# Opening attention's pools and strands inside the recurrence's scheduling loop, one pool at a time

## The chip, the core and the metric

The kernel runs on one core of a Trainium2 chip. It is one launch. The time is that of the device, in microseconds (us), for the whole launch; it is given as the median of three runs. One execution was also profiled, and every row below is from that one. The core's engines each work through their own instructions in order: PE (TensorE, matrix products; PEld are its weight loads), ACT (ScalarE), DVE (VectorE), POOL (GpSimd) and SP (SyncE, which here issues every transfer between memory and the core).

## What is computed

A decoder layer over 528 positions (16 meta tokens and 512 inputs) of width 1024. Cut to what matters here:

```
h      = rms_norm(concat(meta, x)) ; proj = h @ w_in          # 1024 -> 8480 columns
o_rwkv = rwkv7_mix(proj[:, 0:3360]) @ rwkv_w_o                 # 16 heads of 64, a recurrence over time
o_diff = diff_attention(proj[:, 3360:6432]) @ diff_w_o         # 8 heads; each the difference of two causal softmaxes
gates  = sigmoid(proj[:, 6432:8480])                           # 2 x 1024
h_res  = h_res + (gates0 * o_rwkv + gates1 * o_diff) @ w_out
h_res  = h_res + square(relu(rms_norm(h_res) @ mlp_w1)) @ mlp_w2
out    = rms_norm(h_res)[16:]
```

All of it is float32. A wide product is done as three products of rounded halves (high x high, high x low, low x high).

## The kernel before

**Stages.** First the input is normed and turned (lines 130 to 252). Then comes a part whose order is planned by hand (lines 270 to 1525, inside `mstack`): the recurrence and attention. Then the end of attention's output product, the merge, `w_out` and the MLP (from line 1530).

**The planner.** Each piece of work is a Python generator, a *strand*, that yields operations (`Op`, line 282) or conditions to wait for. `run` (line 1125) takes again and again the strand whose next operation could start first by estimated costs and times, with a small handicap by `RANK` (line 1115) and a limit (`debt`) on how much PE work of short bursts may go ahead of dense work. What it picks is written into the engines' queues in that order. The estimates choose the order alone; on the chip each instruction waits for what it really needs. A tile's slot is known to the planner as free at the time in `touched`.

**Dense work.** `loader`, `splitter`, `wide` and `evacuation` (lines 574 to 641) run the wide products: a job is one tile of 128 output columns. `loader` issues the weights in four transfers of two row tiles, `splitter` makes their halves on ACT and POOL (`whi`, `wlo`), `wide` runs the matmuls (tile `fil`) and `evacuation` empties the result. Jobs needed by the recurrence are in `need`; all the others (attention's q, k, v columns and 16 gate jobs) are in `other` and serve as filling between the recurrence's short matmuls. `HELD = 6` (line 531) keeps the last six gate jobs back until `closed[0]` is set.

**The recurrence** goes over four groups of four heads. Of group `grp`, `operands` (line 1102) makes the operands, `substitution` and `inverse` the triangular inverses (done: `inverted[grp]`), `chain` (line 889) the nine steps in series (done: `chained[grp]`), and `finish` (line 1002) norms the result, adds the bonus, multiplies by the gate and stores it to `or_d` (done: `finished[grp]`). Two groups are in work at a time. The pools are `pd`, `pe`, `pr` in SBUF and `psg` (tiles `gm0`, `gm1`), `psr` (`sm`, `py`), `psj` and `psf` in PSUM, two banks each.

**The seam.** `run()` of the recurrence returns when only the four strands of dense work are left (line 1133), which is after `finish` of group 3. All its pools are then closed, attention's pools opened (line 1169), the six held jobs put around the products with `rwkv_w_o` (`job_o`, eight jobs) and `diff_w_o` (`job_d`, eight jobs of half length, over the first four heads), and a second `run(True)` starts with attention's strands (line 1521).

**Attention.** `fetching` (line 1201) loads q, k, v and the rotated rows of a head, `loading` (1233) turns v on PE and makes the halves of q, k and v (done: `H[hd]`); four heads may be loaded and not yet attended. `vf` has one buffer, so the v of a head is loaded after the head before it is done. `scoring` and `softmax` (1291 to 1343) make the scores (`sc`) and their exponentials (`p`), `differences` and `weighting` the weighted values (`attended[hd]`), `norms` the norm and the store to `od_d`. `outs` (1455) reloads the recurrence's result from `or_d` and makes its halves (`oh`, `ol`) for `job_o`, after `soft[3]`; `reloads` (1496) does so for `job_d` (`dh`, `dl`) after the eight `job_o`.

The planner's and the dense work's key lines:

```python
elif len(other) > (0 if closed[0] else HELD):          # 564
    yield other.pop(0)()
...
if not last and all(s[1].gi_code.co_name in LASTING for s in strands):   # 1133
    return
...
other[:] = held[:len(held) - 1] + [lambda m=m: job_o(m) for m in range(NT)] + held[len(held) - 1:] + [...job_d...]   # 1519
closed[0] = True
for g in (setup(), fetching(), loading(), scoring(), differences(), weighting(), norms(), outs(), reloads(), gates_ahead()):
    fork(g)
run(True)
```

Of the kernel before, what the change touches and what calls it, by code (L numbers as in the profile page):

```python
# [10 lines left out]
F32 = mybir.dt.float32  # L11
F32R = mybir.dt.float32r
# [67 lines left out]
def hybrid_layer(ctx: ExitStack, tc: tile.TileContext, ins, out):  # L80
# [99 lines left out]
    psj = pstack.enter_context(tc.tile_pool(name="psj", bufs=1, space=PSUM))  # L180
# [94 lines left out]
    with tc.tile_pool(name="pd", bufs=1) as pd_, tc.tile_pool(name="pe", bufs=1) as pe_, tc.tile_pool(name="pr", bufs=1) as pr_, tc.tile_pool(name="psg", bufs=2, space=PSUM) as psg, tc.tile_pool(name="psr", bufs=2, space=PSUM) as psr:  # L275
# [35 lines left out]
        class Pool:  # L311

            def __init__(self, pool):
                self.pool = pool

            def tile(self, shape, dtype, tag=None, name=None, bufs=1):
                tag = tag or name
                t = self.pool.tile(shape, dtype, tag=tag, name=name, bufs=bufs)
                key = (id(self.pool), tag)
                n = turns.get(key, 0)  # L320
                turns[key] = n + 1
                s = slot_of[t.tensor.name] = (*key, n % bufs)
                fresh[t.tensor.name] = touched.get(s, 0.0)
                return t

        pd_, pe_, pr_, psg, psr, early_, gpool_, psf_, psj_ = (Pool(x) for x in (pd_, pe_, pr_, psg, psr, early, gpool, psf, psj))
# [204 lines left out]
        HELD = 6  # L531
# [357 lines left out]
        def chain(G):  # L889
# [3 lines left out]
            Yg = G["Yg"] = pr_.tile([P, 2, NC - 1, C], F32, tag="Yg", name="Yg")  # L893
# [108 lines left out]
        def finish(grp, G):  # L1002
# [3 lines left out]
            var = pr_.tile([P, 16], F32, tag="var", name="var")  # L1006
            rsh, vs = ([projected[w, grp, pr] for pr in range(2)] for w in "rv")

            def norm(i, n):

                for j in range(0, n, 8):
                    o = 8 * i + j
                    ysq = pr_.tile([P, S], F32, tag="ft", name="ysq", bufs=2).rearrange("p (a b) -> p a b", b=C)
# [10 lines left out]
            def bonus(pr):  # L1024
                r = rsh[pr]
                hi = pr_.tile([P, S], F32R, tag="ft", name="bhi", bufs=2)
                yield act(out=hi, in_=r, func=AF.Copy)
                lo = pr_.tile([P, S], F32R, tag="ft", name="blo", bufs=2)
# [9 lines left out]
            def gate_rows(pr):  # L1038
                g2 = ins["rwkv_g2"][0, :, P * (2 * grp + pr):P * (2 * grp + pr + 1)]
                raw = pr_.tile([P, 2, P], F32, tag="graw", name="graw")  # L1040
# [5 lines left out]
            def gate_halves(raw):  # L1046
                g2h = pr_.tile([P, 2, P], F32R, tag="g2h", name="g2h")
                g2l = pr_.tile([P, P], F32R, tag="g2l", name="g2l")
# [13 lines left out]
            for pr in range(2):  # L1062
# [7 lines left out]
                yf = pr_.tile([P, S], F32, tag="ft", name="yf", bufs=2)  # L1070
# [31 lines left out]
        def operands():  # L1102

            for grp in range(4):
# [11 lines left out]
                "fetching": 1, "loading": 2, "scoring": 1, "softmax": 1, "differences": 1, "weighting": 1, "norms": 2, "merging": 2, "outs": 2, "reloads": 2, "gates_ahead": 2, "setup": 0}  # L1116
        LASTING = ("loader", "splitter", "wide", "evacuation")
# [7 lines left out]
        def run(last=False):  # L1125

            while True:
# [5 lines left out]
                if not last and all(s[1].gi_code.co_name in LASTING for s in strands):  # L1133
                    return
# [26 lines left out]
        for g in (loader(), splitter(), wide(), evacuation(), states(), operands(), endings()):  # L1161
            fork(g)
        run()

    estack.close()
    pstack.close()


    with tc.tile_pool(name="pa1", bufs=1, reuse_waits="tile") as pa1, tc.tile_pool(name="pa2", bufs=1, reuse_waits="tile") as pa2, tc.tile_pool(name="pa", bufs=2, reuse_waits="tile") as pa, tc.tile_pool(name="psa", bufs=1, space=PSUM, reuse_waits="tile") as psa, ExitStack() as ostack:
        with tc.using_default_side("right"):  # L1170
            po = ostack.enter_context(tc.tile_pool(name="po", bufs=1, reuse_waits="tile"))
        pa1, pa2, pa, psa, po = (Pool(x) for x in (pa1, pa2, pa, psa, po))
        BANKS.update(sc=(psa, ("sc0", "sc1", "sc2")), sm=(psa, ("sm0", "sm1")), o=(psa, ("o",)))

        ka = pa1.tile([P, KN - K_CAU], F32, name="ka")
        ones = pa.tile([P, 1], F32, name="ones")
        rope = ka[:, K_COS - K_CAU:KN - K_CAU].rearrange("p (a t) -> p a t", a=2)
        cau, idb = (pa.tile([P, P], BF16, name=n) for n in ("cau", "idb"))


        vms = [pa.tile([P, P], F32R, tag=f"vm{i}", name=f"vm{i}") for i in range(4)]

        kzs = [pa.tile([P, 2, M], F32R, tag=f"kz{i}", name=f"kz{i}") for i in range(4)]
        am = pa.tile([P, 256], F32R, name="am")
        H, soft, sums_of, mixed, turned, attended, normed, heads_out = {}, {}, {}, {}, {}, {}, {}, []

        def setup():
            yield dma(out=ka, in_=ins["consts"][:, K_CAU:KN])
            yield dve("memset", ones, 1.0)
            yield dve("tensor_copy", idb, ident)  # L1190
            for t in vms + [am] + [x.rearrange("p a b -> p (a b)") for x in kzs]:
                yield dve("tensor_scalar", out=t, in0=par[:, 0:1].to_broadcast((P, t.shape[-1])), scalar1=0.0, scalar2=None, op0=ALU.mult)
            yield dve("tensor_copy", cau, ka[:, 0:P])
# [7 lines left out]
        def fetching():  # L1201

            for hp in range(4):
# [7 lines left out]
                yield dve("tensor_tensor", out=xx, in0=xx, in1=rope[:, 0, :], op=ALU.mult)  # L1211
# [521 lines left out]
```

## Time and profile before

| what | us |
|---|---|
| median of 3 runs (1294.82 to 1300.45) | 1298.17 |
| profiled execution | 1297.67 |
| its span, first to last instruction | 1295.6 |
| PE busy | 1202.4 (93%) |
| DVE busy | 704.8 (54%) |
| ACT busy | 646.0 (50%) |
| POOL busy | 401.4 (31%) |

A row of the timeline gives the start, the duration, the engine, the line of the kernel, the operation, what it writes and reads, the shape and how many were merged into the row; in brackets the engine's idle time before it and what ended that. L118, L359, L365 and L373 are lines of helpers, so the tiles' names tell which piece of work it is. "Granted clock" (PEclk) is the share of TensorE's full clock of 2.4 GHz that was granted; it is 1.0 or 0.5 (1.2 GHz), and values between are means over a stretch.

### The profile page before, as it was taken

How to read it: one execution, taken by the hardware profiler on the slowest of the kernel's cores; microseconds unless marked ns; L12 is line 12 of the kernel's file. 1: busy time of each engine (PE TensorE's matmuls, PEld its weight loads, DVE VectorE, ACT ScalarE, POOL GpSimd, SP SyncE). 2: the span in 40 equal slices, each digit the busy share in tenths (PEclk: the TensorE clock that was granted, in tenths of full speed). 3: DMA queues.
4: the chain of work that ended last, by engine and by line, in shares of the span. 5: the costliest groups of instructions: out<-in, count | busy, mean ns of one | idle time of the engine just before them, and what ended most of it. 6: DMA issues, size and time to landing. Idle time of an engine off the chain costs nothing.

```text
span 1295.6 us, 22932 instructions
## 1 busy us (share of the span) xinstructions
PE 1202.4 (93%) x8297; PEld 992.8 (77%) x8297; DVE 704.8 (54%) x1387; ACT 646.0 (50%) x1561; POOL 401.4 (31%) x619
## 2 busy tenths in 40 slices
PE   5999899989999899999687999998899999999997
PEld 5999787878878787776465777776788888888886
DVE  4546845694359845923357877745544332444233
ACT  6675466645656475454277878523344311234222
POOL 3555434542435343533154565520000000000000
PEclk9999899998989899999697999999999999999999
DMA  3322322341224222331564453686233223332222
GB/s 123 88 70 77 91 67 80 91 128 49 60 56 115 57 72 75 103 95 54 145 182 132 148 160 110 224 294 215 81 83 97 98 98 98 98 90 91 96 98 81
DMA packets 166469, 138.18 MB, mean 107 GB/s; under 512 B 12641, under 2 KB 130756, under 8 KB 166356
## 3 DMA queue, kind: packets, MB, share of 16 engines
q1 hardware_dynamic: 166356, 136.73, 35.5%
q8 instruction: 65, 1.06, 0.3%
q14 instruction: 48, 0.39, 0.1%
HBM read 112.36 MB, written 23.23 MB: 105 GB/s over the span
## 4 chain that ended last, share of the span: by engine, by line
PE 59%; DVE 14%; DMA 5%; ACT 4%; issue 3%; SPq 1%; POOL 1%; POOLq 0%; DVEq 0%; ACTq 0%
PE b L118 30%; PE fil L118 18%; PE gm L118 4%; PE sm L118 3%; DVE Tm L365 3%; DVE tmp L365 2%; PE py L118 2%; SPq L373 1%; DMA rl<-th_d 1%; PE sm L394 1%; PE sc L118 1%; DMA xx<-xr_d 1%; PE o L118 1%; DVE mx L365 1%; DVE AR L365 1%
## 5 line engine op out<-in xcount | busy, mean ns | idle before, releaser
L365 POOL TENSOR_TENSOR wlo<-wraw,whi 128x256 fp32r<-128x256 f32 x316 | 249.7, 796 | 346.1 <-ACT whi L359 276.0
L118 PE MATMUL fil<-hh,whi 128*128 128x264 f32 (+2 forms) x880 | 195.0, 326 | 14.2 <-ACT whi L359 9.2
L115 DVE TENSOR_TENSOR wlo<-wraw,whi 128x1024 fp32r<-128x1024 f32 x72 | 88.2, 1224 | 219.6 <-ACT whi L114 219.6
L118 PE MATMUL b<-whi,x 128*128 128x512 f32 x640 | 200.0, 392 | 4.7 <-ACT whi L114 4.7
L114 ACT ACTIVATE whi<-wraw 128x1024 fp32r<-128x1024 f32 x72 | 76.2, 1060 | 251.2 <-PE b L118 234.8
L118 PE MATMUL fil<-hh,wlo 128*128 128x264 f32 (+2 forms) x880 | 192.4, 322 | 0.0
L118 PE MATMUL fil<-hl,whi 128*128 128x264 f32 (+2 forms) x880 | 189.6, 321 | 0.0
L359 ACT ACTIVATE whi<-wraw 128x256 fp32r<-128x256 f32 x316 | 129.0, 413 | 102.6 <-PE fil L118 48.7
L118 PE MATMUL b<-h,whi 128*128 128x512 f32 x512 | 160.6, 395 | 0.8 <-DVE h L1690 0.8
L118 PEld LDWEIGHTS fil<-hh,whi 128*128 128x128 f32 x880 | 136.1, 195 | 28.1 <-ACT whi L359 12.3
L118 PEld LDWEIGHTS b<-whi,x 128*128 128x128 f32 x640 | 120.4, 189 | 31.9 <-ACT whi L114 6.0
L118 PEld LDWEIGHTS fil<-hh,wlo 128*128 128x128 f32 x880 | 135.5, 193 | 11.0 <-POOL wlo L365 0.5
L118 PEld LDWEIGHTS fil<-hl,whi 128*128 128x128 f32 x880 | 135.9, 194 | 10.4 <-issue 0.5
L1670 POOL TENSOR_TENSOR sums<-sums,halfs 128x1 f32<-128x1 f32 x8 | 5.3, 665 | 425.7 <-DVE sums L1669 365.5
L118 PE MATMUL b<-wlo,x 128*128 128x512 f32 x320 | 126.2, 394 | 0.0
L118 PEld LDWEIGHTS b<-h,whi 128*128 128x128 f32 x512 | 96.4, 188 | 23.4 <-DVE h L1690 1.0
L118 PE MATMUL b<-h,wlo 128*128 128x512 f32 x256 | 101.0, 394 | 0.0
L118 PEld LDWEIGHTS b<-wlo,x 128*128 128x128 f32 x320 | 60.6, 189 | 13.9 <-DVE wlo L115 1.1
L365 DVE TENSOR_TENSOR Tm<-Tm,tmp 128x31 f32<-128x31 f32 (+15 forms) x124 | 56.6, 456 | 3.1
L118 PEld LDWEIGHTS b<-h,wlo 128*128 128x128 f32 x256 | 48.3, 188 | 11.3
L365 DVE TENSOR_TENSOR tmp<-Dm,Tm 128x31 f32<-128x31 f32 (+15 forms) x124 | 54.0, 436 | 3.5
L365 DVE COPY suv<-sm 64x128 f32<-64x128 f32 x36 | 10.5, 292 | 73.9 <-ACT suv L359 73.8
(287 smaller groups left out, 2001.4 us busy)
## 6 DMA issues: line engine op xcount, KB each, us to landing
wraw<-in_w_in_dram SPq DMA_DIRECT2D x268, 128.0 KB
wraw<-in_mlp_w_dram SPq DMA_DIRECT2D x64, 512.0 KB
oth<-th_d SPq DMA_DIRECT2D x24, 256.0 KB
th_d<-th SPq DMA_DIRECT2D x16, 256.0 KB
wraw<-in_rwkv_w_o_dram SPq DMA_DIRECT2D x32, 128.0 KB
th_d<-oth SPq DMA_DIRECT2D x16, 256.0 KB
rl<-th_d SPq DMA_DIRECT2D x16, 256.0 KB
wraw<-in_w_out_dram SPq DMA_DIRECT2D x8, 512.0 KB
```

Source lines behind the costliest of these rows:

```text
L114: nc.scalar.activation(out=hi, in_=src, func=AF.Copy)
L115: (lo_eng or nc.vector).tensor_tensor(out=lo, in0=src, in1=hi.bitcast(F32), op=ALU.subtract)
L118: return nc.tensor.matmul(o, lhsT=l, rhs=r, start=start, stop=stop)
L359: lambda: nc.scalar.activation(out=out, in_=in_, func=func, scale=scale, **more), aps(in_, scale, bias), aps(out, accum_out))
L365: return Op(eng, SLOW * (cost or fixed + each * n), lambda: getattr(unit, name)(*args, **kw), aps(*args[1:], *(v for k, v in kw.items() if ...
L373: return Op("SP", 0.45, lambda: nc.sync.dma_start(out=out, in_=in_), aps(in_), [out], 2.4)
L394: self.todo.append(lambda: nc.tensor.transpose(out=o, in_=i, identity=idn))
L1670: nc.gpsimd.tensor_tensor(out=o, in0=o, in1=halfs[:, 0:1], op=ALU.pow)
```

## The change

There is one `run()` now. A strand `opening` closes the recurrence's pools and opens attention's, one after the other:

- After `inverted[3]` and `chained[2]`, that is when the chain of group 3 is about to start, `pd` and `pe` are closed and `pa1` and `pa2` opened in their place; `setup`, `fetching` and `loading` start. `loading` uses the banks `gm0`, `gm1` (was: `sm0`, `sm1` of attention's own pool).
- After `chained[3]`, `pr`, `psj` and `psr` are closed, `pa` and `psa` opened; the held jobs are let go, and scoring, differences, weighting, norms, outs, reloads and gates_ahead start. `finish` of group 3 has its tiles in a pool `pf` that stays and runs beside them.
- `NH = 3` heads may be loaded ahead (was 4), `HELD = 4` (was 6).
- `po` is gone. The halves for `job_o` lie in the recurrence's tiles (`place`), and `outs` starts after `finished[3]` (was `soft[3]`); those for `job_d` lie in attention's input tiles, and `reloads` starts after `H[7]` (was: after the eight `job_o`). Their reload buffer and that of the gates is `ft`, shared with `finish`.
- `pd`, `pe`, later `pa1`, `pa2`, lie on the right side of SBUF. In PSUM `psg` now lies where `psj` lay; `psj` and `psr` are opened after the first stage and marked free for the planner at 5.0.

```diff
-        HELD = 6
+        HELD = 4
...
-            def __init__(self, pool):
-                self.pool = pool
+            def __init__(self, pool=None):
+                self.pool, self.since = pool, 0.0
+
+            def open(self, stack, name, after, **kw):
+                self.pool = stack.enter_context(tc.tile_pool(name=name, bufs=1, reuse_waits="tile", **kw))
+                self.since = max(t for s, t in touched.items() if s[0] in [id(x.pool) for x in after])
...
+        touched[id(psj_.pool), "pj2", 0] = touched[id(psj_.pool), "pj3", 0] = 5.0
...
-                if not last and all(s[1].gi_code.co_name in LASTING for s in strands):
-                    return
...
         def loading():
             for hd in range(8):
-                while hd > 3 and hd - 4 not in attended:
-                    yield until(attended, hd - 4)
+                while hd >= NH and hd - NH not in attended:
+                    yield until(attended, hd - NH)
...
-            pv = yield from bank("sm")
+            pv = yield from bank("gm")
...
+        PLACES = [("vs", PT, 4)] * 4 + [("rsh", S, 4)] * 4 + [("ks", PT, 2)] * 2 + [(n, PT, 1) for n in ("w_hi", "a_hi", "wa_lo")] + [(n, S, 1) for n in ("g_hi", "g_lo", "g_end")]
...
         def outs():
-            yield until(soft, 3)
+            yield until(finished, 3)
             for k in range(NT):
-                t = po.tile([P, S], F32, tag="ol", name="ol", bufs=2)
+                t = pf_.tile([P, S], F32, tag="ft", name="ol", bufs=2)
                 yield dma(out=t, in_=or_d[:, k, :])
-                hi, lo = (po.tile([P, S], F32R, tag=f"o{x}{k}", name=f"o{x}{k}") for x in "hl")
+                hi, lo = place(2 * k), place(2 * k + 1)
...
         def reloads():
-            yield until(gates, *range(NT))
+            yield until(H, 7)
...
+        def opening():
+
+            yield until(inverted, 3)
+            yield until(chained, 2)
+            dstack.close()
+            with tc.using_default_side("right"):
+                pa1.open(astack, "pa1", (pd_, pe_))
+                pa2.open(astack, "pa2", (pd_, pe_))
+            for g in (setup(), fetching(), loading()):
+                fork(g)
+            yield until(chained, 3)
+            while not (dfree[2] and dfree[3]):
+                yield lambda: dfree[2] and dfree[3]
+            rstack.close()
+            bstack.close()
+            pa.open(ostack, "pa", (pr_, pd_))
+            psa.open(ostack, "psa", (psj_, psr), space=PSUM)
+            BANKS.update(sc=(psa, ("sc0", "sc1", "sc2")), o=(psa, ("o",)))
+            assert len(other) == HELD
+            held = other[:]
+            other[:] = held[:HELD - 1] + [lambda m=m: job_o(m) for m in range(NT)] + held[HELD - 1:] + [lambda m=m: job_d(m) for m in range(NT)]
+            closed[0] = True
+            for g in (setup_pa(), scoring(), differences(), weighting(), norms(), outs(), reloads(), gates_ahead()):
+                fork(g)
+
+        for g in (loader(), splitter(), wide(), evacuation(), states(), operands(), endings(), opening()):
             fork(g)
-        run(True)
+        run()
```

## Rows read from the trace of the kernel before

**Rows 1.** The page's 40 slices of 32.4 us: PE's busy tenths, granted clock.
```profile
PE   5999899989999899999687999998899999999997
PEclk9999899998989899999697999999999999999999
```

**Rows 2.** Busy time by stretch: stretch and length; PE, PEld, DVE, ACT, POOL; clock; DMA.
```profile
560.00:610.30 50.30, 49.95 (x513) 34.24 (x512) 13.70 (x45) 26.34 (x80) 16.74 (x31) 1.00 0.23 64
610.30:632.70 22.40, 10.99 (x81) 6.83 (x79) 10.46 (x29) 5.51 (x12) 3.63 (x4) 0.68 0.21 63
632.70:656.70 24.00, 20.75 (x76) 15.43 (x77) 4.83 (x8) 10.46 (x23) 11.37 (x16) 0.87 0.73 215
656.70:720.00 63.30, 53.29 (x276) 38.86 (x274) 50.09 (x117) 49.34 (x134) 30.43 (x48) 0.87 0.48 146
720.00:850.30 130.30, 122.39 (x715) 95.57 (x716) 92.94 (x228) 92.30 (x251) 75.15 (x106) 1.00 0.55 171
850.30:903.00 52.70, 46.36 (x190) 36.14 (x189) 28.42 (x40) 13.83 (x20) 3.05 (x2) 0.97 0.80 271
```

**Rows 3.** Timeline at the seam: the recurrence's last result to the first scores.
```profile
627.90 0.69 DVE L365 TENSOR_TENSOR yf<-gm,yf 128x512 f32<-128x512 f32 x1 [0.60 <-PE gm L118]
632.25 1.03 ACT L359 ACTIVATE whi<-wraw 128x256 fp32r<-128x256 f32 x3 [5.89 <-DMA wraw<-in_w_in_dram]
632.72 1.22 PE L118 MATMUL fil<-hh,whi 128*128 128x512 f32 x2 [4.86 <-ACT whi L359]
641.60 1.84 SPq L373 DMA_DIRECT2D qk<-xx  x3
656.67 0.34 PE L118 MATMUL sc<-k,q 128*128 128x144 f32 x2
```

**Rows 4.** Timeline: chain 2's end, finish 2's end, inverse 3's end, chain 3's end.
```profile
526.66 0.28 ACT L359 ACTIVATE Yg<-py 128x128 f32<-128x128 f32 x1 [0.60 <-PE py L118]
...
564.59 0.34 SPq L373 DMA_DIRECT2D or_d<-yf  x1
...
566.26 1.36 ACT L359 ACTIVATE TT<-Td 32x576 f32<-32x576 f32 x2
...
610.03 0.28 ACT L359 ACTIVATE Yg<-py 128x128 f32<-128x128 f32 x1 [1.25 <-PE py L118]
```

**Rows 5.** Attention's loads: by tile (ns min/median/max, first to last start), and timeline rows.
```profile
L359 ACT ACTIVATE k<-qk x32: 627/642/647, 650.5 to 798.3; 64x528 fp32r<-64x528 f32 x32
L365 POOL TENSOR_TENSOR klo<-qk,k x16: 1292/1323/1665, 651.3 to 800.0; 64x528 fp32r<-64x528 f32 x16
L359 ACT ACTIVATE of<-o x8: 573/588/598, 691.5 to 834.8; 128x512 f32<-128x512 f32 x8
...
782.52 0.20 POOL L365 CAST kz<-klo 64x16 fp32r<-64x16 f32 x1
782.62 0.34 PE L118 MATMUL sc<-k,q 128*128 128x144 f32 x2
784.88 0.63 PE L394 MATMUL sm<-kc,vf 128*128 128x128 f32 x4 [0.25 <-DMA vf<-v_d]
```

**Rows 6.** By tile: the halves of the reloaded results, of `or_d` and of `od_d`.
```profile
L359 ACT ACTIVATE oh<-ol x8: 613/631/638, 682.2 to 713.8; 128x512 fp32r<-128x512 f32 x8
L365 DVE TENSOR_TENSOR ol<-ol,oh x8: 674/687/1775, 682.9 to 714.4; 128x512 fp32r<-128x512 f32 x8
L359 ACT ACTIVATE dh<-ol x4: 629/632/634, 803.4 to 815.1; 128x512 fp32r<-128x512 f32 x4
```

**Rows 7.** Timeline where the planned part meets the next stage.
```profile
849.84 0.61 PE L118 MATMUL fil<-dh,wlo 128*128 128x512 f32 x2
850.29 11.30 PE L118 MATMUL b<-x,xw 128*128 128x512 f32 x48
...
860.42 0.32 SPq L373 DMA_DIRECT2D th_d<-oth  x1
...
863.24 0.96 PE L118 MATMUL b<-x,xw 128*128 128x512 f32 x3 [1.65 <-ACT xw L114]
```

More of the change, by code (lines that the diff above doesn't have):

```diff
@@ L271, in hybrid_layer @@
     mstack.enter_context(tc.manual_schedule())
[L275 removed]
+    fstack, rstack, dstack, bstack, astack, ostack = (ExitStack() for _ in range(6))
+    with fstack:
+        pf_, pr_ = (s.enter_context(tc.tile_pool(name=n, bufs=1)) for s, n in ((fstack, "pf"), (rstack, "pr")))
+        with tc.using_default_side("right"):
+            pd_, pe_ = (dstack.enter_context(tc.tile_pool(name=n, bufs=1)) for n in ("pd", "pe"))
+        psj, psr = (bstack.enter_context(tc.tile_pool(name=n, bufs=1, space=PSUM)) for n in ("psj", "psr"))
         now = {e: 0.0 for e in ("PE", "ACT", "DVE", "POOL", "SP")}
@@ L1123, in fork, with run @@
             strands.append(s)
-        def run(last=False):
+        def run():
             while True:
@@ L1159, in run @@
                 s[2] = next(s[1], None)
[L1161 to L1184, printed above, removed]
@@ L1185, in hybrid_layer @@
+        pa1, pa2, pa, psa = (Pool() for _ in range(4))
+        K = {}
         H, soft, sums_of, mixed, turned, attended, normed, heads_out = {}, {}, {}, {}, {}, {}, {}, []
+        NH = 3
         def setup():
+            ka = pa1.tile([P, KN - K_CAU], F32, name="ka")
+            K["rope"] = ka[:, K_COS - K_CAU:KN - K_CAU].rearrange("p (a t) -> p a t", a=2)
             yield dma(out=ka, in_=ins["consts"][:, K_CAU:KN])
-            yield dve("memset", ones, 1.0)
-            yield dve("tensor_copy", idb, ident)
@@ L1191, in setup @@
-            for t in vms + [am] + [x.rearrange("p a b -> p (a b)") for x in kzs]:
-                yield dve("tensor_scalar", out=t, in0=par[:, 0:1].to_broadcast((P, t.shape[-1])), scalar1=0.0, scalar2=None, op0=ALU.mult)
-            yield dve("tensor_copy", cau, ka[:, 0:P])
+            K["vm"] = [pa2.tile([P, P], F32R, tag=f"vm{i}", name=f"vm{i}") for i in range(NH)]
+            K["kz"] = [pa2.tile([P, 2, M], F32R, tag=f"kz{i}", name=f"kz{i}") for i in range(NH)]
+            K["cau"], K["idb"] = (pa2.tile([P, P], BF16, name=n) for n in ("cau", "idb"))
@@ new lines, in setup, with setup_pa @@
+            yield dve("tensor_copy", K["idb"], ident)
+            for t in K["vm"] + [x.rearrange("p a b -> p (a b)") for x in K["kz"]]:
+                yield dve("tensor_scalar", out=t, in0=par[:, 0:1].to_broadcast((P, t.shape[-1])), scalar1=0.0, scalar2=None, op0=ALU.mult)
+            yield dve("tensor_copy", K["cau"], ka[:, 0:P])
+        def setup_pa():
+            K["ones"] = pa.tile([P, 1], F32, name="ones")
+            K["am"] = pa.tile([P, 256], F32R, name="am")
+            yield dve("memset", K["ones"], 1.0)
+            yield dve("tensor_scalar", out=K["am"], in0=par[:, 0:1].to_broadcast((P, 256)), scalar1=0.0, scalar2=None, op0=ALU.mult)
@@ L1280, in values_a @@
             back(pv)
-            pm = yield from bank("sm")
+            pm = yield from bank("gm")
             b_ = Burst()
@@ L1310, in softmax @@
             if i == 3:
-                end = yield from bank("sm")
+                end = yield from bank("gm")
             b_ = Burst()
@@ L1516, in job_d @@
             return ins["diff_w_o"][0], P * m, (full,), d_hi, d_lo, evac, NS
-        held = other[:]
-        other[:] = held[:len(held) - 1] + [lambda m=m: job_o(m) for m in range(NT)] + held[len(held) - 1:] + [lambda m=m: job_d(m) for m in range(NT)]
-        closed[0] = True
-        for g in (setup(), fetching(), loading(), scoring(), differences(), weighting(), norms(), outs(), reloads(), gates_ahead()):
-            fork(g)
-        run(True)
-    mstack.close()
+        def opening():
+            yield until(inverted, 3)
+            yield until(chained, 2)
+            dstack.close()
+            with tc.using_default_side("right"):
+                pa1.open(astack, "pa1", (pd_, pe_))
[17 more added lines that the diff above has]
+        for g in (loader(), splitter(), wide(), evacuation(), states(), operands(), endings(), opening()):
+            fork(g)
+        run()
+        mstack.close()
+        ostack.close()
+    astack.close()
+    estack.close()
+    pstack.close()
     hstack.close()
```

70 lines of the change are left out of this document (38 added, 32 removed).

## The prediction

> **What bounds the kernel now.** I read the 40 slices first, then the stretches around the dip in them, then the timeline at the seam, then the tiles of attention's loads. In the slices PE is at nine tenths nearly everywhere, and the deepest dip after the start is at slices 20 to 22 (616 to 713 us), where the granted clock falls too [rows 1]. So PE sets the time, and what it loses there is what a change of order can win. The stretches say how much [rows 2]. Up to the end of the last chain, 560.0 to 610.3, PE idles 0.35 us. From 610.3 to 720.0 it idles 11.41 + 3.25 + 10.01 = 24.7 us, and the clock is at half for part of the time: busy time by the missing share of the clock is 10.99 x 0.32 + 20.75 x 0.13 + 53.29 x 0.13 = 13.2 us. From 720.0 to 850.3 it idles 7.9 us at full clock. Over 610.3 to 850.3 that is 45.8 us lost of 240.0, so 194.2 us are work at full clock.
>
> The timeline gives the cause. The recurrence's last product is made at 627.90; until then dense work has nothing, because the held jobs are not let go. Then everything starts with transfers: PE waits until 632.72 for the first halves, these for their weights, and the first scores run only at 656.67 [rows 3], 46.6 us after the last chain's end at 610.03 [rows 4]. Later attention is still paced by its loads: the last k piece of head 6 is done at 782.52 + 0.20 and its scores begin at 782.62 [rows 5].
>
> **The change part by part.** The matmuls are the same before and after, so I count PE's lost time, not its work.
>
> *Two held jobs less.* 48 matmuls of 512 columns; 48 such take 11.30 us [rows 7], so 11.3 us of PE move from behind the chain's end to before it. That is neutral as long as PE is full there, which the idle 0.35 us says [rows 2].
>
> *Loads of heads 0 to 2 beside chain 3.* `opening` can start them at about 567.6, when inverse 3 ends, so they have until 610 or later [rows 4]. PE gets 15 turns, 0.63 us for four [rows 5], 2.4 us. With the two jobs, 13.7 us more PE work stand before the chain's end than did, so the chain may be stretched by that much without idling PE. ACT gets per head four k pieces of 0.642 us and three more of like size, 4.5 us; POOL two of 1.323 us [rows 5]; DVE some five of 0.687 us [rows 6], 3.4 us. ACT was busy 26.34 of 50.30 us there, DVE 13.70, POOL 16.74 [rows 2], so all fit; cost nothing, from a bound of everything in the chain's way (the slower rival) down to nothing. On SP's queue 27 transfers and that of the constants pass between the fill's weights at some 0.6 us each [rows 3], 17 us in 43; the DMA engines are at 0.23 there and were at 0.73 when the same loads came in a rush [rows 2]. Nothing queued behind them is short of time unless one waits for its tile.
>
> *Scores at the chain's end.* No wait for `finish`, no reload of the fill: the 45.8 us are replaced by what a running attention loses. The stretch from 720.0 to 850.3 idles 7.91 us for 122.39 busy, 0.065 [rows 2]; on 194.2 us of work that is 12.5 us. It could be as little as the 0.35 in 50 of the chain (1.4 us) or more at the start.
>
> *The start.* `finish` of group 3 now shares the engines and the banks `gm0`, `gm1` with attention's turns. Alone it took from 610.03 to 628.6, 18.6 us; beside other work the one before took 526.66 to 564.59, 37.9 us [rows 3, 4]. `outs` waits for it (was: after four softmaxes), and behind that wait stands `job_o`, 45 us of fill. The three held jobs (16.9 us) and `finish`'s own PE work (10.99 us at clock 0.68, 7.5) must cover the time with attention. I take 6 us of idle, between 0 and the gap of the rival below. In the old dip 24.7 us of idle came with 13.2 us lost to the clock, 0.53 per us; so 6 x 1.53 = 9.2 us.
>
> *Three heads ahead, not four.* Head 7's load took from 784.88 to about 801.5 (the last k piece starts at 800.0 and takes 1.3) [rows 5], 16.6 us; it would wait for head 4. Heads are attended between 691.5 and 834.8, 20.5 us apart [rows 5], so a load begun three heads ahead is done in time. Nothing; if that cover fails, each of five heads waits.
>
> *`reloads` after `H[7]`.* That is at about 801.5 and the first half of it was made at 803.4 already [rows 6]; nothing. *The halves' new places, the two buffers `ft`, setup's move, the PSUM order*: the same instructions; nothing.
>
> *The next stage.* Its first tiles now lie on memory that `pf` and `pa` use to the end; before, on attention's inputs, free long ago. It began at once at 850.29 and later waited 1.65 us for a split [rows 7]. If a tile waits for the last store of the gates at 860.42, PE has 12 matmuls (2.8 us) and then idles some 7 to 9 us; between 0 and 9 I take 1.65 x 1.53 = 2.5 us, as only few of the tiles lie on a buffer used that late.
>
> **Sum.** 45.8 lost before; 12.5 + 9.2 + 2.5 = 24.2 after; 21.6 us gained. The profiled execution took 1297.67 us (span 1295.6 and 2.1 around it), 0.5 under the median of 1298.17: 1297.67 - 21.6 = 1276.1.
>
> **A rule beside a row.** The stretch of the chain has PE busy 49.95 of 50.30 us but weight loads 34.24, a share of 0.68, where running attention has 95.57 of 130.30, 0.73 [rows 2]. The Trainium skill (Perfetto Trace Analysis, Identifying the Most-Contended Engine) says that matmul busy time is a poor measure of how full PE is and that the weight loads' share is a good one. By that there is room in the chain; what it would give is the second rival.
>
> **The rivals.**
>
> *The fill runs out before `job_o` is ready.* From the chain's end to the first halves: 37.9 us and some 5 for reload and split, 43. Cover: 16.9 + 7.5, and attention's own work. The fill of 632.7 to 850.3 is 6 x 24 + 8 x 24 + 8 x 12 = 432 matmuls, 101.7 us, of 186.8 us of work; the other 85.1 in the 193.6 us from the first scores are 0.44, in 43 us 18.9. Sum 43.3: just enough. If attention at its start does half of that, 9.5 us more idle, 14.5 with the clock: 1291. For it: attention's chain from scores to values was long (the first head's scores at 656.67, its values at 691.5 [rows 3, 5]). Against: three loaded heads instead of one.
>
> *The chain has room.* Then the moved 13.7 us cost nothing where they go: 1276.1 - 13.7 = 1262. Against it: the 0.35 us of idle.
>
> *Slower: the loads stretch chain 3.* It took 566.26 to 610.03, 43.8 us for nine steps in series [rows 4], each through PE, ACT and DVE; an operation of a load ahead of a step's own delays it. All of them in the way: 3 x (4.5 + 2.6 + 3.4) = 31.5 us, 13.7 covered by PE's extra work, 17.8 idle, 27.2 with the clock: 1303. They can also lengthen one another: a DVE subtraction of 687 ns reached 1775 and a POOL one of 1323 reached 1665 in the crowded start of attention [rows 5, 6]; half of 1.1 us on 15 more makes the stretch 40 us and the time 1316. It is slower than before from a stretch of 13.7 + 21.6 / 1.53 = 28 us, 3.1 us a step. Against it: ACT and DVE are about half and a quarter busy there. The Trainium skill speaks for it (SBUF — State Buffer, Who interferes with whom): a VectorE instruction with two inputs in SBUF contends with a GpSimd one that reads SBUF, as these subtractions are. The long outliers agree; no row here shows which instruction met which.
>
> *Nothing comes of it.* The order lets attention in, but the first loads or exponentials wait on the chip for the recurrence's tiles beneath them, and the start is only shifted: about 1297.
>
> **How the numbers follow.** Forecast 0.52, fill gap 0.18, room in the chain 0.08, nothing 0.10, slower 0.12. About 0.5% (6.5 us) is what a measurement of this kernel can tell from no change, so faster means under 1291.7 and slower over 1304.7: faster 0.77 (the first three, less a little of the gap), same 0.11, slower 0.12. The range goes from 1260 (room in the chain; the forecast without attention's idle is 1265) to 1300 (the gap and nothing within it); the slower case stays out.
>
> **What would show it.** Right: the first scores within 15 us of the last chain's end, three heads' k pieces before it, PE's idle and half clock between the chain's end and the last `job_d` under 30 us together, the planned part done some 20 us sooner. The chain may end up to 14 us later and that costs nothing. Wrong: PE idle inside chain 3; a hole between the last held job and the first `job_o`; SP standing at a load while weights queue behind it; a wait of PE at the start of the next stage beyond 9 us.

## The result and the profile after

The changed kernel takes 1285.40 us (median of 5, 1282.81 to 1289.29) against 1300.45 us before (5 runs beside them): ratio 0.989, interval 0.986 to 0.992, so 15 us faster. The forecast was 1276.1: right in sign and inside the range, 9.3 us too low.

The profiled execution of that measurement was the longest of its five, 1289.29 us. The kernel was profiled again beside the first experiments, in an execution of 1285.57 us (span 1283.8); "the changed kernel" below is that one. The page's slices of PE and granted clock, 32.1 us each, to be held against [rows 1]:

```profile
PE   4998899999999899989899999679899999999997
PEclk9998899999999999999999999989999999999999
```

The dip at 616 to 713 us is gone. There is another at slices 26 and 27 (802 to 867 us), and the first slice has fallen from 5 to 4. The stretches put numbers on it. In each row: start and end, length, then busy time (and instructions) of PE, PEld, DVE, ACT, POOL, the clock, DMA. Both kernels are cut at the same events: 45 us; the end of inverse 3; chain 3's end; the last product of the planned part; about 60 us into the next stage; the end. First the kernel before, then the changed one:

```profile
0.00:45.00 45.00, 31.83 (x230) 29.83 (x231) 20.07 (x55) 28.91 (x64) 17.71 (x34) 1.00 0.36 110
45.00:567.60 522.60, 493.64 (x4632) 430.96 (x4632) 330.66 (x688) 298.00 (x815) 239.83 (x376) 0.97 0.30 82
567.60:610.30 42.70, 42.34 (x441) 28.58 (x439) 11.12 (x39) 22.27 (x72) 14.92 (x27) 1.00 0.20 54
610.30:850.50 240.20, 207.62 (x1146) 156.87 (x1145) 158.52 (x381) 157.81 (x418) 120.58 (x172) 0.92 0.52 159
850.50:910.30 59.80, 53.46 (x221) 41.95 (x220) 31.73 (x44) 18.05 (x30) 3.05 (x2) 0.97 0.74 246
```
```profile
0.00:45.00 45.00, 26.82 (x169) 24.73 (x170) 17.59 (x49) 24.43 (x52) 12.51 (x26) 0.92 0.32 98
45.00:569.90 524.90, 496.93 (x4685) 434.92 (x4684) 337.85 (x700) 302.22 (x825) 244.87 (x385) 0.97 0.31 81
569.90:620.90 51.00, 47.64 (x463) 33.20 (x462) 20.83 (x57) 32.84 (x94) 24.33 (x40) 0.97 0.55 155
620.90:827.10 206.20, 192.19 (x1131) 147.96 (x1129) 153.05 (x351) 143.38 (x392) 114.48 (x158) 0.99 0.51 153
827.10:901.70 74.60, 58.62 (x243) 46.62 (x243) 35.17 (x49) 21.59 (x36) 2.52 (x2) 0.89 0.67 223
```

From such rows comes the account that the rest of this text uses: PE's loss in a stretch is its idle time plus what the halved clock took from its busy time. (The clock is summed matmul by matmul, since the mean over a stretch also counts half clock while PE is idle; over the 240 us before that would give some 3 us too much.) E4 is the best kernel below.

| stretch | before | changed | E4 |
|---|---|---|---|
| to 45 us | 13.2 | 21.3 | 13.3 |
| to the end of inverse 3 | 43.2 | 40.1 | 36.4 |
| chain 3 | 0.4 | 5.1 | 5.9 |
| chain 3's end to the last planned product | 46.2 | 15.7 | 23.3 |
| from there some 60 us into the next stage | 8.1 | 18.2 | 4.2 |
| rest | 11.8 | 13.4 | 11.8 |
| sum of losses | 122.8 | 113.8 | 94.9 |
| span | 1295.6 | 1283.8 | 1265.5 |

What is left of a span after its losses is PE's work at full clock: 1172.8, 1170.0 and 1170.6 us. So the change gains 30.5 us where it was meant to, gives back 8.1 at the start, 4.7 in chain 3 and 10.1 at the next stage, and the other stretches and the work make up the rest. The second stretch differs between executions of the same instructions: it lost 42.2 us in the first profile of the changed kernel, and E2, E4 and E10, which run the same operations in the same order up to there, lost 40.6, 36.4 and 42.0. So the 3.1 us between 43.2 and 40.1 are not clear of noise.

**The seam that was to go.** The timeline shows the end of inverse 3, chain 3's end, the first scores and the last store of `finish` 3, as [rows 3, 4] did:

```profile
568.53 1.36 ACT L370 ACTIVATE TT<-Td 32x576 f32<-32x576 f32 x2
620.66 0.28 ACT L370 ACTIVATE Yg<-py 128x128 f32<-128x128 f32 x1 [0.94 <-PE py L118]
621.12 0.34 PE L118 MATMUL sc<-k,q 128*128 128x144 f32 x2
665.56 0.34 SPq L384 DMA_DIRECT2D or_d<-yf  x1
```

The scores begin 0.5 us after the chain's last result, where it was 46.6 us. `finish` 3, beside attention, takes 45 us instead of 18.6.

**A new hole at the end.** The last product of the planned part, the last store of the gates, and what follows it on SP, ACT and PE; before, PE went on at once [rows 7]:

```profile
826.48 0.62 PE L118 MATMUL fil<-dhalf,wlo 128*128 128x512 f32 x2
834.38 0.32 SPq L384 DMA_DIRECT2D th_d<-oth  x1
834.75 0.43 SPq L92 DMA_DIRECT2D wraw<-in_diff_w_o_dram  x1
839.97 1.15 ACT L114 ACTIVATE xw<-wraw 128x512 fp32r<-128x512 f32 x2 [16.90 <-DMA wraw<-in_diff_w_o_dram]
841.03 1.13 ACT L114 ACTIVATE x<-rl 128x512 fp32r<-128x512 f32 x2
841.69 4.66 PE L118 MATMUL b<-x,xw 128*128 128x512 f32 x10 [14.59 <-ACT x L114]
```

PE idles 14.59 us. The first weights of the next stage are issued 0.37 us behind the last store of the gates. Until that store only the gates' own last operations run; PE has nothing left to do.

**A new hole at the start.** SP's queue in the kernel before, then SP's queue and PE in the changed one:

```profile
15.75 1.21 SPq L373 DMA_DIRECT2D raw<-in_rwkv_w_dram  x2
```
```profile
25.64 1.21 SPq L384 DMA_DIRECT2D raw<-in_rwkv_w_dram  x2
28.24 6.47 SPq L384 DMA_DIRECT2D wraw<-in_w_in_dram  x6
31.08 1.25 PE L118 MATMUL fil<-hh,whi 128*128 128x264 f32 x4 [5.33 <-ACT whi L370]
```

The load of `raw` was issued at 15.75 us before and stands now until 25.64; the fill's weights stand behind it, PE idles 5.33 us, and its granted clock is at half from 30.4 to 37.2 us.

### The profile page after: what moved, and what is told of

Read it like the earlier page. It is cut to its first block, busy times and chain, and to the rows that moved or that the text cites. A ratio compares the mean times of both kernels' runs of the same rounds, so it can differ in the third digit from the quotient of the medians.

```text
span 1287.5 us, 22900 instructions
## 1 busy us (share of the span) xinstructions
PE 1196.2 (93%) x8297; PEld 991.2 (77%) x8297; DVE 716.6 (56%) x1385; ACT 646.4 (50%) x1561; POOL 403.4 (31%) x619
## 4 chain that ended last, share of the span: by engine, by line
PE 58%; DVE 21%; DMA 7%; ACT 5%; issue 4%; POOL 2%; SPq 2%; POOLq 0%; ACTq 0%; DVEq 0%
PE b L118 29%; PE fil L118 18%; DVE Tm L376 4%; PE gm L118 4%; DVE tmp L376 4%; PE sm L118 3%; PE py L118 2%; DMA rl<-th_d 2%; SPq L384 2%; PE gm L405 1%; DVE AR L376 1%; DMA wraw<-in_diff_w_o_dram 1%; DMA oth<-th_d 1%; ACT p L370 1%; DMA wraw<-in_w_in_dram 1%
## 5 line engine op out<-in xcount | busy, mean ns | idle before, releaser
L118 PE MATMUL fil<-hh,whi 128*128 128x264 f32 (+2 forms) x880 | 197.4, 327 | 13.1 <-ACT whi L370 7.3
L118 PE MATMUL fil<-hl,whi 128*128 128x264 f32 (+2 forms) x880 | 193.2, 322 | 0.0
L118 PEld LDWEIGHTS fil<-hh,wlo 128*128 128x128 f32 x880 | 135.9, 193 | 10.6 <-issue 0.3
L118 PEld LDWEIGHTS b<-wlo,x 128*128 128x128 f32 x320 | 60.1, 188 | 13.2 <-DVE wlo L115 0.6
L118 PEld LDWEIGHTS b<-h,wlo 128*128 128x128 f32 x256 | 48.6, 190 | 11.5
```

What stands on the lines that cost most here:

```text
L118: return nc.tensor.matmul(o, lhsT=l, rhs=r, start=start, stop=stop)
```

## Experiments

**E0. The changed kernel again**, as the measure for E1 to E3.

> The changed kernel itself, beside the three below. 1285 us, 15 us under the kernel before (ratio 0.989), with the first scores about 0.5 us after the last chain's end at about 623 us and two holes of PE: 5.5 us at about 31 us, and 14.7 us ahead of the first product of the next stage at about 845 us.

1284.06 us, ratio 0.988 (0.986 to 0.990). The rows above are its own.

**E1. The next stage's memory moved up.**

```diff
+    pad = ctx.enter_context(tc.tile_pool(name="pad", bufs=1, reuse_waits="tile"))
+    pad.tile([P, 6800], F32, name="pad")
     wc0, wc = (ctx.enter_context(tc.tile_pool(name=n, bufs=1, reuse_waits="tile")) for n in ("wc0", "wc"))
```

> The changed kernel with the memory of the next stage (weights, halves and od rows of the second half of diff_w_o) moved up by 27 KB per partition, off pf and pa; every instruction is the same. Theory: the 14.7 us hole exists because these tiles lie on memory that attention's pools hold to the end, so the first weights come behind the last store of the gates. Moved, the first weights are issued some 20 us ahead of that store, the hole falls to about 1.7 us as in the kernel before, and 14.7 - 1.7 + 2.0 us of lost clock = 15 us go: 1270 us, ratio 0.978. The part after the hole, 442 us in the changed kernel against 445 before, may give 3 us of it back: 1273. Rival: the hole only stands where the next stage waits for the gates' rows anyway, so that its end comes no sooner: 1282 to 1286.

1279.86 us, ratio 0.984 (0.982 to 0.987): 4 us, not 15. The rows say why:

```profile
800.30 0.48 SPq L92 DMA_DIRECT2D wraw<-in_diff_w_o_dram  x1
839.04 0.32 SPq L384 DMA_DIRECT2D th_d<-oth  x1
839.05 1.67 ACT L114 ACTIVATE x<-rl 128x512 fp32r<-128x512 f32 x3 [1.36 <-POOL oth L376]
839.73 2.80 PE L118 MATMUL b<-x,xw 128*128 128x512 f32 x5 [9.22 <-ACT x L114]
```

The weights now come 39 us ahead of the last store, so where the tiles lie does decide when they are loaded. But the halves `x` of the `od_d` rows had been moved onto the ring `oth`, and wait for its last use. The move was too short; and the last store came at 839.0 instead of 834.4.

**E2. `raw` elsewhere.**

```diff
-            raw = pr_.tile([P, 2, P], F32, tag="raw", name="raw")
+            raw = gpool_.tile([P, 2, P], F32, tag="raw", name="raw")
```

> The changed kernel with the one tile raw (the low rank weights of a pair) in gpool instead of pr. Theory: SP stands at its load from 15.8 to 25.5 us because pr lies on the first stage's pool, with the fill's weights behind it, and PE idles 5.5 us at 31 us and loses 3.0 us to the clock. Without the wait 7 to 8.5 us go: 1277 us, ratio 0.983. Rival: the recurrence's first group sets the time there, and an idle PE early only means that the fill ends later: 1284 to 1286, the same as the changed kernel.

1275.37 us, ratio 0.981 (0.979 to 0.983): 8.7 us for the place of one tile of 1 KB per partition. SP's queue is that of the kernel before again:

```profile
15.62 1.21 SPq L384 DMA_DIRECT2D raw<-in_rwkv_w_dram  x2
19.48 13.17 SPq L384 DMA_DIRECT2D wraw<-in_w_in_dram  x8
```

The loss to 45 us falls from 21.3 to 12.8, and all of it arrives at the end: a hole 780 us ahead of the seam isn't made good by anything.

**E3. Both edits.**

> Both edits, raw elsewhere and the next stage moved. If both theories hold the gains add, as the holes are 800 us apart: 1285 - 15 - 7.5 = 1263 us, ratio 0.971. If only the hole at the end counts 1270; if only the one at the start 1277; if neither 1285.

1274.78 us, ratio 0.980 (0.977 to 0.982). Beside E2 the move of E1 brings nothing that can be told from none. The hole at the end is 9.3 us as in E1, and the next stage loses 11.5 us instead of the 16.1 of E2; but attention loses 22.4 instead of 16.3, and that is half clock (6.2 us instead of none) and not idle time (16.2 and 16.3).

**E4. The next stage clear of attention's last tiles.** On top of E2:

```diff
-    wc0, wc = (ctx.enter_context(tc.tile_pool(name=n, bufs=1, reuse_waits="tile")) for n in ("wc0", "wc"))
+    wc2 = ctx.enter_context(tc.tile_pool(name="wc2", bufs=1, reuse_waits="tile"))
+    pad = ctx.enter_context(tc.tile_pool(name="pad", bufs=1, reuse_waits="tile"))
+    pad.tile([P, 4160], F32, name="pad")
+    wc = ctx.enter_context(tc.tile_pool(name="wc", bufs=1, reuse_waits="tile"))
+    wc0 = ctx.enter_context(tc.tile_pool(name="wc0", bufs=1, reuse_waits="tile"))
...
-    wc2 = ctx.enter_context(tc.tile_pool(name="wc2", bufs=1, reuse_waits="tile"))
```

> The kernel with raw elsewhere (1275.4 us), and the next stage's pools opened in another order with a gap between them, so that its weights, its od rows and the halves of these rows all lie off pf and pa. With the smaller move of e1 the hole only fell from 14.6 to 9.2 us: the weights came early, but the halves x of the od rows still stood on the ring oth and were split behind the last store, and the last job_d's ran 4.6 us slower with the next stage's instructions between theirs on the queues. Theory: with x clear too the hole falls to 1 to 3 us and 6 to 8 us go against the 1274.8 of both edits: 1267, ratio 0.974. Rival: the last job_d's lose on DVE, POOL and SP what the hole gives, as these queues run in order: 1272 to 1276.

1267.65 us, ratio 0.976 (0.973 to 0.980), the best of all: 31 us under the kernel before.

```profile
800.28 0.43 SPq L92 DMA_DIRECT2D wraw<-in_diff_w_o_dram  x1
824.12 22.47 PE L118 MATMUL b<-x,xw 128*128 128x512 f32 x96
831.01 0.32 SPq L384 DMA_DIRECT2D th_d<-oth  x1
819.71 1.83 PE L118 MATMUL fil<-dhalf,whi 128*128 128x512 f32 x4 [1.80 <-ACT x L114]
```

The next stage begins at 824.12, 7 us ahead of the last store of the gates, and runs 96 matmuls with no wait. The rival was right about a part: the loss from there falls from 16.1 us in E2 to 4.2, but that of attention rises from 16.3 to 23.3. Of these 7.0 us, 4.9 stand in the last 20 us of the planned part, where the next stage's instructions now lie between the last `job_d`'s on the queues: PE idles 6.7 us there instead of 5.0, 1.80 of it behind a split `x` on ACT (the last row), and loses 3.2 to the clock instead of none. The rest goes with two spells of half clock at 659.5 and 686.8 us, far ahead of the edit; of such spells the changed kernel has one in one profile and two in the other. At the seam itself, then, 11.9 us are gained and 4.9 given back. The medians differ by 7.7, but E4's profiled execution also lost 4.2 us less than E2's ahead of chain 3, which the edit does not touch: the sign is clear, the size only to within some us.

**E5. The loads only behind chain 3.**

```diff
             yield until(chained, 2)
+            yield until(chained, 3)
             dstack.close()
```

> The changed kernel with one line more: the constants, the loads and the splitting of heads begin only when chain 3 has ended, not when inverse 3 has. Scores, held jobs and banks stay. Theory A, the early loads are the gain: the first scores come some 27 to 29 us after the chain's end, as in the kernel before, attention sets the end, and the planned part ends 19 us later: 1303 us, ratio 1.00. Theory B, PE is what sets the time and the held jobs and finish cover 24.4 us of the wait: 5 us of idle and what the clock loses with them, 1290 to 1294, ratio 0.994. If the loads had slowed chain 3, it ends some us sooner than 622 by more than the 2.4 us of their turns on PE.

1311.71 us, ratio 1.010 (1.007 to 1.012): slower than before, theory A and beyond it. Chain 3, then its end to the last planned product:

```profile
568.60:612.00 43.40, 43.28 (x444) 29.30 (x443) 12.22 (x48) 23.24 (x74) 16.45 (x31) 1.00 0.27 70
612.00:851.30 239.30, 210.18 (x1150) 160.52 (x1148) 154.26 (x366) 154.41 (x411) 122.80 (x169) 0.93 0.51 154
```

The second row is the kernel before once more: 239.3 us long and 45.5 lost there, against 240.2 and 46.2. Held jobs let go, `finish` beside attention and scores at 642.21 instead of 656.67 are worth nothing without the early loads; and the costs at both ends remain, so the kernel is slower. The first row gives the loads' price: chain 3 lasts 43.4 us without them and 51.0 with them, and PE's loss in it is 0.1 against 5.1; the other 2.6 us are matmuls, 10 turns of v and 9 of the fill. In the other profiles with the same loads the chain lasts 48.8 to 51.6 us.

**E6. The scores only behind `finish` 3.**

```diff
         def scoring():
+            yield until(finished, 3)
             for n in range(32):
```

> The changed kernel with one line more: the scores wait until finish of group 3 is done; loads stay beside the chain. Theory A, running attention beside finish is worth its length: finish alone takes 18.6 us instead of some 42, the first scores come 20 us later than at 621 to 623 us, and the kernel is 10 to 20 us slower: 1295 to 1305. Theory B, what counts is that PE has work: the three held jobs (16.9 us) and finish's own 7.5 us cover 24.4 us, finish is done sooner and job_o with it, and the time stays within 4 us of the changed kernel: 1282 to 1289.

1307.03 us, ratio 1.007 (1.004 to 1.009): theory A. In the profiled execution, at 1311.35 us the longest of the 12, `finish` takes 41 us instead of 45 and not 18.6, as the heads' loads and the held jobs run beside it; the first scores come at 662.98, and from chain 3's end to the last planned product 39.6 us are lost instead of 15.7:

```profile
623.00:852.50 229.50, 205.61 (x1131) 157.68 (x1129) 149.51 (x351) 143.81 (x391) 111.48 (x158) 0.93 0.46 139
```

So it takes both halves of the change: heads loaded when the chain ends, and scores that start then.

**E7. Six held jobs.** `HELD = 6` in the place of 4.

> The changed kernel with six held jobs instead of four, so 11.3 us of dense work go from before the end of chain 3 to behind it. Theory: the chain ended 13 us later than in the kernel before because PE was given 13.7 us more work ahead of its end, at no cost; with six it ends at 611 to 613 us and the time does not move: 1283 to 1287. Rival: the loads on ACT, DVE and POOL stretched the chain; then it ends at 618 or later with PE idle before it, and the time is up to 11 us longer: 1290 to 1296.

1294.52 us, ratio 0.997 (0.995 to 0.999). My theory fell in both its parts. The rival was right about the chain: it ends at 621.0, as with four, so the loads stretch it and not moved work. The rival's time came out too, but by another way. Work from the start to chain 3's end, for the kernel before, the changed one and this one:

```profile
0.00:610.30 610.30, 567.81 (x5298) 489.37 (x5299) 361.85 (x781) 349.18 (x950) 272.46 (x437) 0.97 0.30 82
```
```profile
0.00:620.90 620.90, 571.38 (x5312) 492.85 (x5313) 376.26 (x805) 359.50 (x971) 281.71 (x451) 0.97 0.33 89
```
```profile
0.00:621.00 621.00, 570.04 (x5315) 492.13 (x5316) 376.99 (x806) 360.66 (x969) 281.49 (x449) 0.98 0.33 89
```

The changed kernel has 14 matmuls more than the kernel before ahead of that point, 10 turns of v, for two heads, and 4 matmuls of the fill. The 48 of two held jobs never went there, with 4 held or with 6 (143 and 144 matmuls of `w_in` come behind the chain's end, and 147 in the kernel before; six jobs are 144): with 4 held the loader has taken up those jobs by then, but their matmuls come behind the chain all the same. And the time still rises by 10 us. Here `finish` 3 ends 9 us later (its last store at 674.28), the reloads with it, and the first `job_o` starves:

```profile
686.66 0.86 PE L118 MATMUL fil<-half,whi 128*128 128x512 f32 x3
700.84 1.75 PE L118 MATMUL fil<-half,whi 128*128 128x512 f32 x4
711.14 1.63 PE L118 MATMUL fil<-half,whi 128*128 128x512 f32 x3
```

From 690 to 710 PE idles 7.9 us of 20 here and 2.0 in the changed kernel; with the clock, 685 to 721 loses 11.1 here and 4.9 there: 6.2 of the 11.4 us that E7 loses more between the chain's end and the last planned product (27.1 instead of 15.7). That is the gap of the first rival. In the changed kernel it is avoided narrowly: the last held product is at 685.1 and the first `job_o` at 688.6. Why the order made by the planner puts `finish` later with six held jobs I did not find out.

**E8. Two heads ahead.** `NH = 2`.

> The changed kernel with two heads loaded ahead instead of three (and two of each of their buffers). Theory on the chain: the loads beside it cost it 7.6 us (51.0 us with them, 43.4 without), a third per head; with two heads it lasts 48 to 49 us and ends 2 to 3 us sooner. Theory on attention: a head's load takes 16.6 us and heads are attended some 20 us apart, so with two ahead the load of each is still done in time, and what is lost is under 5 us: 1281 to 1290. Rival: the third head is what attention lives on at its start (its scores would wait for head 0 to be attended at 653 us and then for a load of 17 us and more beside finish), and each later head waits some us: 1300 or more.

1297.34 us, ratio 0.998 (0.996 to 1.000): 12 us given up, between theory and rival. PE loses 25.4 us instead of 15.7 in attention, and the results of the heads come later:

```profile
L370 ACT ACTIVATE of<-o x8: 583/592/599, 649.3 to 821.3; 128x512 f32<-128x512 f32 x8
```

The last is at 821.3, against 801.1 in the changed kernel: with two ahead the loads pace attention again. The theory on the chain was not tested. In the changed kernel, too, only two heads are split before the chain ends, and the third is turned after it; first the changed kernel, then E8:

```profile
L370 ACT ACTIVATE k<-qk x8: 640/642/644, 590.9 to 614.4; 64x528 fp32r<-64x528 f32 x8
621.78 0.61 PE L405 MATMUL gm<-kc,vf 128*128 128x128 f32 x4
```
```profile
L370 ACT ACTIVATE k<-qk x8: 640/642/643, 593.5 to 617.0; 64x528 fp32r<-64x528 f32 x8
650.71 0.65 PE L405 MATMUL gm<-kc,vf 128*128 128x128 f32 x4
```

Eight k pieces are two heads, in both chains, and both have 463 matmuls; they last 51.0 and 50.2 us. What E8 moves is the third head's load, 29 us later, to where the rival put it.

**E9. Waits tile by tile in `pf` and `pr`.**

```diff
-        pf_, pr_ = (s.enter_context(tc.tile_pool(name=n, bufs=1)) for s, n in ((fstack, "pf"), (rstack, "pr")))
+        pf_, pr_ = (s.enter_context(tc.tile_pool(name=n, bufs=1, reuse_waits="tile")) for s, n in ((fstack, "pf"), (rstack, "pr")))
```

> The changed kernel, with the pools pf and pr told to wait tile by tile (as the pools of attention are) instead of for all that lay beneath the pool; raw stays where it is, on the bytes of the first stage's input. Theory: what cost 8 us at the start is that raw's load waited for the last user of any tile of the first stage's pool; waiting only for the users of its own bytes it is issued at about 16 to 20 us instead of 25.5, and the time is that of the kernel with raw elsewhere: 1275 to 1278. Rival: the bytes of raw are themselves used late, and it makes no difference: 1284.

1280.42 us, ratio 0.985 (0.983 to 0.988), in the middle of both. The profiled execution is the longest of the five, 1289.05 us; what follows is from its first 45 us. The load is issued 1.3 us sooner than in the changed kernel, and the loss to 45 us is 17.6 us instead of 21.3:

```profile
24.37 1.21 SPq L384 DMA_DIRECT2D raw<-in_rwkv_w_dram  x2
```

The wait that ends last is now PE's turns of the input (the longest on SP there, 8.2 us) and no longer DVE's `lam` (9.6 us): the bytes of `raw` themselves lie on rows of the input that are read late. So the granularity of the wait was the smaller part (1.3 of the 9.9 us that the load comes late, 3.7 us of loss where E2 took away 8.5) and the place the larger, as in E2.

**E10. The second pair of heads rotated later.** On top of E4:

```diff
+                if hp:
+                    yield until(chained, 3)
                 yield dve("tensor_tensor", out=xx, in0=xx, in1=K["rope"][:, 0, :], op=ALU.mult)
```

> The kernel with both seams mended (raw elsewhere, next stage clear, 1267.65 us), in which the three DVE operations that rotate q and k of the second pair of heads wait for the end of chain 3. In that kernel the seventh step of the chain takes 8.0 us instead of 5.1: these three (1.01, 0.71, 0.71 us) and two subtractions for q stand on DVE ahead of the step's own instruction. Theory: the step goes back to 5 or 6 us, chain 3 to 47 to 49 us from 51.5, ends 2 to 4 us sooner, and the time falls by what the chain loses there, 2 to 4 us: 1265, ratio 0.974. Rival: the third head is then ready later than its scores want it (the second head's begin 13.6 us after the chain's end, the third's 33 us), or its rotation delays the first softmaxes on DVE, and attention loses as much or more: 1268 to 1275.

1281.36 us, ratio 0.987 (0.983 to 0.990): 14 us slower than E4. The seventh step did not get shorter (9.1 us), so DVE was not what stretched it. The same place in E4 and then here, ACT's queue and the step's product:

```profile
596.51 1.62 ACT L370 ACTIVATE suv<-py 64x128 f32<-64x128 f32 x5
598.24 0.45 PE L118 MATMUL sm<-suv,KB 128*64 128x64 f32 x8
```
```profile
602.77 1.31 ACT L370 ACTIVATE k<-qk 64x528 fp32r<-64x528 f32 x2
604.00 1.32 ACT L370 ACTIVATE suv<-py 64x256 f32<-64x256 f32 x4
604.21 0.45 PE L118 MATMUL sm<-suv,KB 128*64 128x64 f32 x8
```

In E4 the product starts 0.1 us after the last of five copies `suv` on ACT, here 0.2 us after the first of four began, behind two copies of k. That looks like a wait for ACT, but PE does not wait there. The busy time of the fill alone (tile `fil`), from the step's product before (`sm<-x,TT`) to this one, in the kernel before, E4 and E10:

```profile
598.35:600.08 1.73, 1.42 (x6) 1.00 0.00 0
593.73:598.24 4.51, 4.00 (x16) 1.00 0.60 131
599.71:604.21 4.50, 3.99 (x16) 1.00 0.36 94
```

PE is busy for the whole of each stretch, from product to product. The stretch is 2.8 us longer than in the kernel before, 2.6 of it fill that stands ahead of the product in PE's own queue, in the order that the planner wrote: nearly all of 8.0 against 5.1 us. Only behind the product does PE wait, 1.1 us for DVE in E4 and 0.7 us for ACT here. Whether the product would have waited for ACT without this fill, no run shows. What the edit did show is the price behind the chain: from its end to the last planned product PE loses 33.7 us instead of 23.3, and the last store of `finish` comes 58 us after the chain's end instead of 45. That is 10 of the 14 us; the profiled execution also lost 5.6 us more than E4's ahead of chain 3, where both run the same operations.

## Why the prediction was right, and where 9 us went

Of the signs that were named for being right, all came but one: two heads' k pieces were made before the chain's end, not three. Of the four for being wrong, three came as well: PE idle in chain 3 (3.4 us), SP standing at a load with weights behind it (`raw`, 9.9 us), and a wait at the next stage beyond 9 us (14.59). The last two are where the 9 us went.

**What bounds the kernel, and the seam: right.** The loss around attention was put at 45.8 us and its rest at 12.5 + 9.2 = 21.7. (The three clock terms of the 45.8 add up to 13.1 and not 13.2; summed matmul by matmul they are 13.6, and the loss is 46.2.) It is 15.7 behind the chain and 4.7 more in the chain, 20.4. E5 and E6 show that it is this mechanism: with one half undone all of the gain behind the chain goes, with the other 24 of its 30 us.

**Two held jobs and turns, "13.7 us more PE work stand before the chain's end": wrong.** 14 matmuls more stand there. The chain did end 10.6 us later, as "up to 14 us later" allowed, but for other reasons: inverse 3 ends 2.3 us later, behind the start's hole, and the chain is 8.3 us longer. Of the 10.6 us 9.7 are loss, and hardly any is work that was moved. That the chain's loss hardly shows in the sum is luck: the loss behind the chain was 6.0 us smaller than forecast.

**Loads beside chain 3, "cost nothing": mis-sized.** E5 gives 7.6 us of length and 5.0 us of PE, and that for two heads: the third was priced beside the chain and came behind it (E8). The slower rival had the right kind of cost at the wrong size: 28 us was the point from which it would have decided. The durations stay near [rows 5, 6] (a `klo` 1.30 to 1.54 us, a subtraction for q 0.69), so no instruction got much longer. What got longer is the line ahead of a step's operations, in the longest step that of the fill on PE (E10); what share each engine's line has in the 7.6 us, no run shows. The Trainium skill's rule on VectorE and GpSimd sharing a port (SBUF — State Buffer, Who interferes with whom) is not what these rows show.

**Room in the chain (the second rival): no sign of it.** Per us of chain 3, PE makes 444 / 43.4 = 10.2 matmuls without the loads and 463 / 51.0 = 9.1 with them. By the weight loads' share of 0.68 there would have been room (the Trainium skill, Perfetto Trace Analysis, Identifying the Most-Contended Engine); the rows speak against it here. The two jobs never went there, so no run tried it in full.

**The start of attention, 6 us of idle: right in kind, too high.** Up to the first `job_o` PE idles 4.6 us in 68, about the rate of running attention, so most of the term's 9.2 us did not come. The fill gap came within 3.5 us of opening, and E7 shows it open.

**Three heads ahead: right.** E8 shows that two cost 12 us; whether four would be better was not tried.

**The next stage, 2.5 us between 0 and 9: wrong size.** It lost 18.2 us instead of 8.1. The step said that few of its tiles lie on a buffer used late and that PE would still have 12 matmuls. All of the first tiles lay on attention's pools: the weights came behind the last store, PE had none of those matmuls, and the way from the last product over the gates' last operations (7.3 us to the store) and the weights' transfer (7.3 us to the first product) lay open. That is 10.1 us where 2.5 were forecast, and 14.59 us of idle where the step's own bound was 9.

**"The halves' new places, two buffers, setup's move, the PSUM order: nothing": wrong.** `pr` was moved onto the memory of the first stage's input, and the first load into it waited for the last user of that stage's pool (DVE's `lam`), with the fill's weights behind it: 8.1 us in the account, 8.7 in E2. The diff shows the pool's new place as plainly as the next stage's; I traced the memory at one end only. The two terms are 15.7 us too small. The profiled executions differ by 11.8 us where 21.6 were forecast, 9.8 less: 3.1 less loss before inverse 3, 1.7 more gained around chain 3 and attention (25.8 instead of 24.1) and 2.8 less work came off the 15.7, and 1.6 in the rest came on top. The 3.1 are within what that stretch varies by, and so are the 2.8: over the changed kernel's variants, which all compute the same, the work comes out between 1167.1 and 1172.2 us.

## What to carry to other kernels

When a change moves pools, list for each new pool what lay on its bytes and who reads that last, at every stage border and not only where the change aims; the first load of a stage and the queue behind it pay for it. Here a tile of 1 KB per partition was worth 8.7 us and the order of three pools some 7, together about as much again as the change had gained. And an overlap is worth its full price only with both halves: loads early enough and work that starts when they are there.

## What I had not expected of the hardware

A wait on SP's queue alone set PE back by 8 us at the start, and nothing later made good for it, with PE at nine tenths all the way: E2 gained 8.7 us for 8.5 us of loss taken away. The 14.6 us of idle at the end cost little on the clock: it was at half from 829.1 to 846.2 us, but PE was idle for most of that, and only 2.3 us of busy time were lost. In the prediction each us of idle took another 0.53 with it, from the seam before; here it was 0.15.
